# Another order of the first nine pieces and their products in the opening of a matmul with layer norm

## The chip, the core and the metric

The kernel runs on one core of one Trainium2 chip. The metric is the device time of one execution in microseconds (us); lower is better. Its engines are named as the profile names them: PE is TensorE (PEld its weight loads), DVE is VectorE, ACT is ScalarE, POOL is GpSimd, SP is SyncE, which here only issues DMAs.

## What is computed

`a` and `b` are 2048 x 2048, single precision; `gamma` and `beta` have 2048 elements.

```python
x = np.matmul(a, b)
mean = np.mean(x, axis=-1, keepdims=True)
var = np.var(x, axis=-1, keepdims=True)
normalized = (x - mean) / np.sqrt(var + eps)
return (gamma * normalized + beta).astype(np.float32)
```

## The kernel before, in words

The output is cut into 16 row tiles of 128 rows and 4 column quarters of 512. The contraction is cut into 16 k tiles of 128; four of them make a chunk. A product (`mm`, L85) is one 128x128 by 128x512 matmul in half precision, which adds one k tile to one bank of PSUM, the accumulator of one row tile and one quarter. In all there are 16 x 4 x 16 = 1024 products.

The single-precision inputs come by DMA from SP's queue into staging tiles (pool `stg`, six of them) and are cast to half precision by DVE: a piece of `a` (128 rows x 512 columns, 256 KB) by `load_a1` (L184 the DMA, L186 the cast), a piece of `b` (one k tile x one quarter, 256 KB) by `load_b1` (L198, L199), and doubled pieces of 512 KB by `load_a2` (L190, L194) and `load_b2` (L203, L205). Two single pieces share a staging tile, in the order in which they are loaded. SP waits, before a later load, until the staging tile is free and until the DMA eight places ahead of it has landed.

A piece of `a` has to be turned before it can be the stationary side of a product. `turn` (L243, L245) does four PE transposes of 128x128 into a bank of PSUM and one ACT copy from there into the tile `at`.

**The opening** works on the first five row tiles (R = 5) while the inputs come in. It takes quarter 0 of chunk 0 first (nine single pieces: A0 to A4 of `a`, B0 to B3 of `b`), then quarters 1 and 2 of chunk 0, then quarter 3 (`MAIN`) over all chunks, then the rest of quarters 0 to 2. The sums over chunk 0 of the first three quarters are copied out of PSUM by ACT (`put_aside`, L261) and added back later. After the opening, row tiles 5 to 15 are done one after the other: four quarters of 16 products each, with the layer norm of an earlier row on DVE beside them.

**What sets the order.** The kernel runs under a manual schedule: every engine does its instructions in the order in which the program calls them. The list `arrivals` sets the order of the nine DMAs on SP's queue and of their casts on DVE. The calls of `turn`, `mm` and `put_aside` set the order on PE and on ACT. In the kernel before, the arrivals are A0 B0 A1 A2 A3 A4 B1 B2 B3, and PE does, after the first row tile:

- turn row tiles 1, 2, 3 and 4, each as its piece arrives, and between them the products of k tile 0 for row tiles 1, 2 and 3
- k tile 1 for row tiles 0 to 3
- k tiles 0 and 1 for row tile 4
- k tile 2 for row tiles 0 to 4, then k tile 3 for row tiles 0 to 4; behind each product of k tile 3 ACT puts that row tile's sum aside

Before the first piece arrives, and in the first waits, PE multiplies zeros (`filler`, L236).

Of the kernel before, what the change touches and what calls it, by code (L numbers as in the profile page):

```python
# [16 lines left out]
def kernel(  # L17
# [19 lines left out]
    KC = 4  # L37
    KW = KC * P
    n_kc = n_kt // KC
    R = 5  # L40
# [32 lines left out]
    def bank(name):  # L73
        return psum.tile([P, NB], FP32, tag="ps", name=name)
# [4 lines left out]
    def at(i):  # L79
        return pair[i // 2][:, i % 2]  # L80

    def mm(i, q, kt, first, last):
        if (i, q) not in acc:
            acc[i, q] = bank(f"acc{i}_{q}")
        nc.tensor.matmul(  # L85
            acc[i, q], at(i)[:, kt, :], b16[:, kt, ds(q * NB, NB)],
            start=first, stop=last,
        )
# [71 lines left out]

    arrivals = [("a", 0), ("b", 0)] + [("a", i) for i in range(1, R)]
    arrivals += [("b", k) for k in range(1, KC)]

    a16_of = {}
    fresh = {"st": 0}
# [66 lines left out]
    def filler(n, to=None):  # L234
        for _ in range(n):
            nc.tensor.matmul(warm if to is None else to, zeros[:, 0:P], zeros, start=True, stop=True)  # L236

    def turn(rows, c):
        n = len(rows)
        t_ps = psum.tile([P, n, KC, P], FP16, tag="ps", name=f"tps{rows[0]}_{c}")  # L240
        for m, i in enumerate(rows):
            for j in range(KC):
                nc.tensor.transpose(t_ps[:, m, j, :], a16_of[i, c][:, ts(j, P)], ident)  # L243
        i0 = rows[0]
        nc.scalar.copy(  # L245
            pair[i0 // 2][:, ds(i0 % 2, n), ds(c * KC, KC), :], t_ps)
# [10 lines left out]
    def put_aside(p, q):  # L257
        if xs[p] is None:
            xs[p] = xpool.tile([P, N], FP32, tag="x", name=f"x{p}")
            bnst[p] = stat.tile([P, n_nb, 6], FP32, tag="bnst", name=f"bnst{p}")  # L260
        nc.scalar.copy(xs[p][:, ds(q * NB, NB)], acc.pop((p, q)))  # L261
# [11 lines left out]
    filler(1)  # L273
    turn([1], 0)
    filler(2)
    for i in range(2, R):
        turn([i], 0)
        mm(i - 1, 0, 0, True, False)
    for p in range(R - 1):
        mm(p, 0, 1, False, False)  # L280
    mm(R - 1, 0, 0, True, False)
    mm(R - 1, 0, 1, False, False)
    for kt in range(2, KC):
        for p in range(R):
            mm(p, 0, kt, False, kt == KC - 1)
            if kt == KC - 1:
                put_aside(p, 0)


    for q in ASIDE[1:]:  # L290
# [198 lines left out]
```

## Time and profile before

| | |
|---|---|
| device time, three runs | 245.38, 245.78, 245.42 us; median 245.42 us |
| the profiled execution's own time | 245.69 us |
| its span, first to last instruction | 243.70 us |
| so outside the span | 1.99 us |
| mean granted TensorE clock | 0.991 |
| DVE busy | 173.0 us (71%) |
| ACT busy | 55.1 us (23%) |
| DMA traffic in the opening's stretch 10 to 12 us | 383 GB/s |

Times inside an execution are counted from the span's start. A line of the timeline has the start, the duration, the engine, the line of the program, the operation with its tiles, and the number of merged instructions; what stands in brackets is the idle time of the engine before it and what ended it. The duration of a matmul is modelled and pipelined: a product of 512 columns is shown with 0.38 us, though the next one starts 0.22 us after it. So the start to start time is the one to count with. The chain of waits is the chain of work that ended last, in order of time.

### The profile page before, as it was taken

The page shows a single profiled execution, that of the slowest core. Times are in us where ns is not written, and L with a number is a line of the kernel's source. Part 1 is how long each engine was busy: PE and PEld are TensorE (multiplying, and loading weights), DVE is VectorE, ACT ScalarE, POOL GpSimd, SP SyncE. Part 2 cuts the span into 40 slices and gives each one's busy share as a digit, 9 for nine tenths or more (in the row PEclk, how much of TensorE's full clock was granted, in tenths as well). Part 3 has the DMA queues.
Part 4 walks back from the last instruction along what each step waited for, and adds up shares of the span by engine and source line. Part 5 has one row for each costly group of instructions (what it writes and reads, how often), then busy time and mean ns, then how long its engine had stood idle before and what let it go on. Part 6 is the DMA issues. An engine that isn't in the chain of part 4 may idle for free.

```text
span 243.7 us, 2983 instructions
## 1 busy us (share of the span) xinstructions
PE 235.0 (96%) x1137; PEld 108.3 (44%) x1137; DVE 173.0 (71%) x304; ACT 55.1 (23%) x104; POOL 12.6 (5%) x19
## 2 busy tenths in 40 slices
PE   6899999999999999999999999999999999999991
PEld 2344555444444444444444444444444444444440
DVE  1544454969997679999999995937558392946771
ACT  2466445500000011112121211112111121112132
POOL 0000000000210100000000000036000000000000
PEclk9999999999999999999999999999999999999996
DMA  4999999999999998888999797683907145120405
GB/s 122 393 389 384 384 350 392 386 335 370 360 266 204 150 139 242 237 186 251 241 224 256 143 290 177 192 202 74 256 5 180 78 115 146 58 114 0 175 1 172
DMA packets 41190, 52.64 MB, mean 216 GB/s; under 512 B 24404, under 2 KB 24404, under 8 KB 40920
## 3 DMA queue, kind: packets, MB, share of 16 engines
q1 hardware_dynamic: 39592, 46.68, 59.1%
q0 software_dynamic: 1584, 5.77, 15.3%
q8 instruction: 9, 0.15, 0.3%
q14 instruction: 5, 0.04, 0.1%
HBM read 35.67 MB, written 16.78 MB: 215 GB/s over the span
## 4 chain that ended last, share of the span: by engine, by line
PE 93%; DMA 2%; ACT 1%; DVE 1%; SPq 0%; issue 0%
PE acc L85 91%; DMA st<-in_a_dram 2%; PE tps L243 2%; ACT x L408 1%; DVE bnst L373 0%; PE y L396 0%; DVE a16s L186 0%; PE warm L236 0%; SPq L198 0%; SPq L184 0%; PE ms_ps L391 0%; ACT mv_last L389 0%; DVE mv_last L388 0%; ACT lead L392 0%
## 5 line engine op out<-in xcount | busy, mean ns | idle before, releaser
L85 PE MATMUL acc<-b,at 128*128 128x512 f16 x1024 | 223.2, 379 | 1.0 <-DVE b L199 0.9
L85 PEld LDWEIGHTS <-at 128*128 128x128 f16 x1024 | 99.6, 98 | 119.3 <-ACT at L245 1.3
L96 DVE BATCH_NORM_STATS2 bnst<-x 128x6 f32<-128x512 f32 x48 | 32.9, 689 | 33.9 <-ACT x L95 33.8
L95 ACT COPY x<-acc 128x512 f32<-128x512 f32 x48 | 27.7, 588 | 108.8 <-PE acc L85 107.5
L117 DVE SCALAR_TENSOR_TENSOR x<-x,rstd,beta_b 128x512 f32<-128x512 f32 x62 | 43.8, 747 | 0.6
L111 DVE SCALAR_TENSOR_TENSOR x<-x,mv,gamma_b 128x512 f32<-128x512 f32 x60 | 42.0, 741 | 0.0
L205 DVE CAST b<-stb 128x1024 f16<-128x1024 f32 x30 | 20.4, 688 | 11.0 <-DMA stb<-in_b_dram 10.9
L106 ACT ACTIVATE sq<-ve 128x1 f32<-128x1 f32 x15 | 3.0, 203 | 51.1 <-DVE ve L104 51.1
L245 ACT COPY at<-tps 128x512 f16<-128x512 f16 (+1 forms) x14 | 10.6, 769 | 14.3 <-PE tps L243 14.0
L265 DVE TENSOR_TENSOR x<-acc,x 128x512 f32<-128x512 f32 x15 | 10.3, 685 | 3.3 <-PE acc L85 3.3
L345 POOL DMA_DIRECT2D a<-in_a_dram x11 | 6.4, 583 | 91.1 <-DMA at<-a 90.8
L266 DVE BATCH_NORM_STATS2 bnst<-x 128x6 f32<-128x512 f32 x15 | 10.4, 695 | 0.5
L261 ACT COPY x<-acc 128x512 f32<-128x512 f32 x15 | 7.6, 607 | 5.1 <-PE acc L85 5.1
L186 DVE CAST a16s<-st 128x512 f16<-128x512 f32 x8 | 3.4, 427 | 6.4 <-DMA st<-in_a_dram 6.2
L243 PE MATMUL tps<-ident,a16s 128*128 128x128 f16 x80 | 6.8, 220 | 0.9 <-DVE a16s L186 0.8
L236 PE MATMUL warm<-zeros 128*128 128x512 f16 x19 | 6.2, 462 | 1.2 <-DVE zeros L152 1.2
L243 PEld LDWEIGHTS <-a16s 128*128 128x128 f16 x80 | 5.2, 98 | 4.7 <-DVE a16s L186 2.6
L194 DVE CAST a16s<-sta 128x1024 f16<-128x1024 f32 x6 | 4.2, 694 | 4.1 <-DMA sta<-in_a_dram 3.4
L357 POOL TENSOR_SCALAR gb<-gb 1x1024 f32<-1x1024 f32 x2 | 5.5, 2764 | 0.0
L102 DVE BATCH_NORM_AGGREGATE mv<-bnst 128x2 f32<-128x24 f32 x15 | 4.0, 264 | 0.5
L236 PEld LDWEIGHTS <-zeros 128*128 128x128 f16 x19 | 2.0, 115 | 4.2 <-issue 2.6
L255 POOL COPY gate<-stb 128x1 f32<-128x1 f32 x1 | 0.2, 183 | 63.5 <-DMA stb<-in_b_dram 63.5
(31 smaller groups left out, 22.8 us busy)
## 6 DMA issues: line engine op xcount, KB each, us to landing
stb<-in_b_dram SPq DMA_DIRECT2D x30, 512.0 KB, 6.5
out_dram<-x SPq DMA_DIRECT2D x30, 512.0 KB, 3.0
a<-in_a_dram POOLq DMA_DIRECT2D x11, 512.0 KB, 6.7
sta<-in_a_dram SPq DMA_DIRECT2D x6, 512.0 KB, 6.3
st<-in_a_dram SPq DMA_DIRECT2D x8, 256.0 KB, 7.4
st<-in_b_dram SPq DMA_DIRECT2D x4, 256.0 KB, 6.6
gamma_b<-in_gamma_dram SPq DMA_DIRECT2D x1, 1024.0 KB, 7.2
beta_b<-in_beta_dram SPq DMA_DIRECT2D x1, 1024.0 KB, 9.2
```

The source lines that it names most:

```text
L85: nc.tensor.matmul(acc[i, q], at(i)[:, kt, :], b16[:, kt, ds(q * NB, NB)], start=first, stop=last,)
L95: nc.scalar.copy(xs[i][:, qs], acc[i, q])
L96: nc.vector.bn_stats(bnst[i][:, q, :], xs[i][:, qs])
L111: nc.vector.scalar_tensor_tensor(xs[i][:, qs], xs[i][:, qs], mv[:, 0:1], gamma_b[:, qs], AluOp.subtract, AluOp.mult)
L117: nc.vector.scalar_tensor_tensor(xs[i][:, qs], xs[i][:, qs], rstd, beta_b[:, qs], AluOp.mult, AluOp.add)
L205: nc.vector.tensor_copy(b16[:, k:k + 2, ds(q * NB, NB)], st)
L236: nc.tensor.matmul(warm if to is None else to, zeros[:, 0:P], zeros, start=True, stop=True)
L243: nc.tensor.transpose(t_ps[:, m, j, :], a16_of[i, c][:, ts(j, P)], ident)
L245: nc.scalar.copy(pair[i0 // 2][:, ds(i0 % 2, n), ds(c * KC, KC), :], t_ps)
L261: nc.scalar.copy(xs[p][:, ds(q * NB, NB)], acc.pop((p, q)))
L265: nc.vector.tensor_tensor(xs[p][:, qs], acc[p, q], xs[p][:, qs], AluOp.add)
L266: nc.vector.bn_stats(bnst[p][:, q, :], xs[p][:, qs])
```

## The change

The arrivals become A0 B0 A1 A2 A3 B1 B2 A4 B3: row tile 4's piece goes from the sixth to the eighth place, and B1 and B2 each come one place earlier. B3 stays ninth.

On PE, everything up to the product of row tile 2 with k tile 0 stays as it is. From there the new order is: k tile 1 for row tiles 0 to 2; k tiles 0 and 1 for row tile 3; k tile 2 for row tiles 0 to 2; the turn of row tile 4; k tile 2 for row tile 3; k tile 3 for row tiles 0 to 3, each put aside at once; and last the four products of row tile 4, which is then put aside. The number of products, transposes, copies, casts and DMAs is the same, and so is all that follows the chunk.

```diff
-    arrivals = [("a", 0), ("b", 0)] + [("a", i) for i in range(1, R)]
-    arrivals += [("b", k) for k in range(1, KC)]
+    arrivals = [("a", 0), ("b", 0)] + [("a", i) for i in range(1, R - 1)]
+    arrivals += [("b", 1), ("b", 2), ("a", R - 1), ("b", 3)]
...
-    for i in range(2, R):
+    for i in range(2, R - 1):
         turn([i], 0)
         mm(i - 1, 0, 0, True, False)
+    for p in range(R - 2):
+        mm(p, 0, 1, False, False)
+    for kt in (0, 1):
+        mm(R - 2, 0, kt, kt == 0, False)
+    for p in range(R - 2):
+        mm(p, 0, 2, False, False)
+    turn([R - 1], 0)
+    mm(R - 2, 0, 2, False, False)
     for p in range(R - 1):
-        mm(p, 0, 1, False, False)
-    mm(R - 1, 0, 0, True, False)
-    mm(R - 1, 0, 1, False, False)
-    for kt in range(2, KC):
-        for p in range(R):
-            mm(p, 0, kt, False, kt == KC - 1)
-            if kt == KC - 1:
-                put_aside(p, 0)
+        mm(p, 0, 3, False, True)
+        put_aside(p, 0)
+    for kt in range(KC):
+        mm(R - 1, 0, kt, kt == 0, kt == KC - 1)
+    put_aside(R - 1, 0)
```

## The prediction, made before the changed kernel ran

> **What bounds the kernel now.** I read the page first: which engine is busy, and who holds the chain that ended last.
>
> ```profile
> PE 235.0 (96%) x1137; PEld 108.3 (44%) x1137; DVE 173.0 (71%) x304; ACT 55.1 (23%) x104; POOL 12.6 (5%) x19
> ...
> PE 93%; DMA 2%; ACT 1%; DVE 1%; SPq 0%; issue 0%
> ```
>
> PE holds 93% of the chain. A busy PE alone proves little, so I went to the chain of waits in order of time (start, us, what), to see where PE begins to be the bound.
>
> ```profile
> 9.87 0.39 PE acc L85
> 10.26 0.29 PE tps L243 x4
> 10.54 14.68 PE acc L85 x67
> 25.22 0.45 PE tps L243 x8
> ...
> 38.72 195.77 PE acc L85 x907
> ```
>
> From 9.87 us on only PE stands in the chain until its last product. The last line gives the pace: 195.77 / 907 = 0.2158 us per product; eight transposes take 0.45 us, so the four of a turn 0.22. The waits on PE from 10 to 234 us list no wait over their limit. But 67 products at 0.2158 make 14.46 us, not 14.68, so small gaps hide in the first stretch. I read them from PE's timeline in narrow windows:
>
> ```profile
> 9.87 0.39 PE L85 MATMUL acc<-b,at 128*128 128x512 f16 x1
> 10.15 0.40 PE L243 MATMUL tps<-ident,a16s 128*128 128x128 f16 x4
> 10.53 0.39 PE L85 MATMUL acc<-b,at 128*128 128x512 f16 x1
> 10.82 0.38 PE L85 MATMUL acc<-b,at 128*128 128x512 f16 x1
> ...
> 14.27 0.59 PE L85 MATMUL acc<-b,at 128*128 128x512 f16 x2
> ```
>
> These are row tile 2's product with k tile 0 (9.87), the turn of row tile 4 (10.15), row tile 3's product with k tile 0 (10.53), the first product of k tile 1 (10.82), and the first of quarter 1 (14.27), with which the changed stretch is over. What each waited for is in DVE's timeline, the casts of A3, A4, B1, B2, B3 and of the first doubled piece:
>
> ```profile
> 8.97 0.43 DVE L186 CAST a16s<-st 128x512 f16<-128x512 f32 x1 [0.24 <-DMA st<-in_a_dram]
> 9.66 0.43 DVE L186 CAST a16s<-st 128x512 f16<-128x512 f32 x1 [0.26 <-DMA st<-in_a_dram]
> 10.33 0.43 DVE L199 CAST b<-st 128x512 f16<-128x512 f32 x1 [0.25 <-DMA st<-in_b_dram]
> 11.01 0.43 DVE L199 CAST b<-st 128x512 f16<-128x512 f32 x1 [0.25 <-DMA st<-in_b_dram]
> 11.67 0.43 DVE L199 CAST b<-st 128x512 f16<-128x512 f32 x1 [0.23 <-DMA st<-in_b_dram]
> 13.03 0.69 DVE L205 CAST b<-stb 128x1024 f16<-128x1024 f32 x1 [0.93 <-DMA stb<-in_b_dram]
> ```
>
> DVE stands idle before each: landings set the pace, one piece per 0.66 to 0.69 us, while PE needs 0.2158 per product. The turn of row tile 4 starts 0.06 after A4's cast ends (10.09), k tile 1 starts 0.06 after B1's (10.76).
>
> **The change, step by step.**
>
> *What PE loses now.* From 9.87 to 14.27 are 4.40 us. In them start 18 products (row tiles 2 and 3 with k tile 0, 4 of k tile 1, 2 of row tile 4, 5 and 5 of k tiles 2 and 3) and one turn: 18 x 0.2158 + 0.22 = 4.11. So 0.29 us is idle, at three places: before the turn of row tile 4 (9.87 + 0.22 = 10.09, starts 10.15: 0.06), behind it, where row tile 3's product waits for ACT's copy of row tile 3 (10.15 + 0.22 = 10.37, starts 10.53: 0.16), and before k tile 1 (10.75 to 10.82: 0.07).
>
> *The moved loads.* Nine DMAs of 256 KB stay nine, in pairs on the same staging tiles; B3 stays ninth and alone, the tenth DMA waits for the same landing as now, and nothing behind is moved past anything. No trace shows a B piece as sixth. The steps between starts of casts are 0.67 and 0.69 (A to A), 0.67 (A4 to B1), 0.67 and 0.66 (B to B); the far row is A0 to B0 with 1.98 (4.94 to 6.93), which would make one piece 1.31 late, and the best row is 0.01 below 0.67. I take the row of the same switch in the running stream, A4 to B1: places six to nine keep their times, 9.66, 10.33, 11.01 and 11.67.
>
> *The new order, ready against needed* (ready is the cast's end plus 0.05):
> - B1 in the sixth place: 9.66 + 0.43 + 0.05 = 10.14; PE is free at 10.09. A wait of 0.06, the only one I find.
> - Row tile 3's copy: its product started at 10.53 as soon as it could; now it is needed at 10.14 + 3 x 0.2158 = 10.79. Cover 0.26.
> - B2: ready 10.82, needed after five products, 11.22. Cover 0.40.
> - A4, eighth: ready 11.01 + 0.48 = 11.49, needed at 11.87. Cover 0.38.
> - B3: ready 11.67 + 0.48 = 12.15, needed after the turn and one product, 11.87 + 0.22 + 0.22 = 12.31. Cover 0.15.
> - Row tile 4's weights: the turn starts at 11.87; ACT's copy started 0.43 after the turn before (10.15 to 10.58) and took 0.58: 12.88, plus 0.05 is 12.93. Needed after four products of k tile 3, 13.17. Cover 0.24.
> - Four products of row tile 4 end the chunk at 13.17 + 0.86 = 14.03, where the first doubled piece is ready (13.03 + 0.69 + 0.05 = 13.77). Cover 0.26.
>
> *Queued behind.* On ACT the copy of row tile 4 now stands just ahead of the puts aside. They start at about 12.88 instead of 13.60 (ACT's timeline) and, at 0.48 apart, four are done before 15. A bank from them is first needed at 14.03 + 6 x 0.2158 = 15.33. Nothing waits. On DVE and SP the order by place is the same.
>
> *Sum.* 14.03 against 14.27: the idle time falls from 0.29 to 0.06, a gain of 0.23 us. Does it reach the end? Behind 14.27 every wait by PE either moves with PE or is for a load. The load with the least cover that I found is `b`'s k tile 12 of quarter 3: the cast ends at 38.67 and PE comes at 39.20.
>
> ```profile
> 37.98 0.69 DVE L205 CAST b<-stb 128x1024 f16<-128x1024 f32 x1 [0.80 <-DMA stb<-in_b_dram]
> ...
> 39.20 0.38 PE L85 MATMUL acc<-b,at 128*128 128x512 f16 x1
> ```
>
> With 0.05 for the start, 0.48 of cover, of which the change uses 0.23. It holds. Against its own time the profiled execution would go from 245.69 to 245.46. The median of the runs shown is 0.27 below that execution, so the same gain is taken from it: 245.42 - 0.23 = **245.19 us**.
>
> *A rule against it.* All the products behind 10.82 start 0.2158 us apart. The Trainium skill (TensorE: Matmul & The Clock Gate, Back-to-back issue gap) gives about 131 ns per matmul of 512 columns as the sustained pace in a stream of weight loads and matmuls. By that figure PE would wait for the arrivals in both orders and be through with the chunk before 13.77 us, so that the sum would be no gain at all. The trace disagrees with it, with 0.2158 us over 907 products.
>
> **The rivals.**
>
> *The gain is eaten later: 245.42.* If the loads of the main stretch run 0.48 us later than in this profile, relative to PE, both kernels wait at k tile 12 for the same landing and the gain is gone; from 0.25 later on part of it goes. For it: the DMAs run full there. Against: the steps of the landings are steady within 0.03 us.
>
> *The cover of B3 is spent: slower.* Now B3 is ready at 12.15 and used at 13.19 (14.27 - 5 x 0.2158), a cover of 1.04; afterwards it is 0.15, with eight products behind it instead of five. A B3 that lands d us later costs the kernel before nothing up to d = 1.04 and the new one d - 0.15. From d = 0.39 on the change loses. One piece late, 0.67: 0.67 - 0.15 - 0.23 = 0.29 slower, 245.71. At the far row, 1.31 late: 246.35. For it: A0 to B0 shows that a piece of `b` can be 1.31 late. Against: that is the queue's start, and six steps behind it hold 0.67.
>
> *The arrivals set the end of the chunk: 245.42.* If a product took 0.18 us or less, the kernel before would have its 16 products behind 10.82 done when the first doubled piece is ready (10.82 + 16 x 0.18 = 13.70, ready 13.77), the new one too, and both would start quarter 1 there. Against: the pace of 0.2158 in the chain. This is what the page's figure would bring about.
>
> *More than forecast.* All the idle time that the order can reach is 0.29: 245.13.
>
> **How the numbers follow.** 0.2% is 0.49 us, about what a measurement of this kernel can tell from no change. The forecast is below it, and so is the gain of all idle time. Chances: forecast 0.78, gain eaten later 0.09, arrivals at the chunk's end 0.01, B3's cover spent 0.07, more than forecast 0.05. The runs shown lie 0.40 apart, so I add half of that, 0.20, at both ends: 245.13 - 0.20 = 244.93, and 245.42 + 0.20 = 245.62. The rival at 245.71 and above stays outside. Faster by over 0.2% (below 244.93) comes only from scatter on top of the gain: 0.09. Slower (above 245.91) needs B3 late by 0.87 us or more, or scatter: 0.06. Within: 0.85.
>
> **What would show it.** In PE's timeline k tile 1 starts at about 10.14, the turn of row tile 4 at 11.87, k tile 3 at 12.31, row tile 4's products at 13.17 and quarter 1 at 14.03. In the chain the stretch from about 10.14 to the next turn is gapless, and the turn that now starts at 25.06 comes at 24.83. The casts in DVE's timeline keep their starts by place. Wrong it would be if k tile 3 waits on its cast, if row tile 4's weights wait on ACT, or if quarter 1 starts at 14.03 and PE gives the 0.23 back before 39 us.

## The result, and the profile after

| | before | after |
|---|---|---|
| median of 22 runs each | 245.46 us | 245.09 us |
| lowest to highest | 245.20 to 246.50 | 244.93 to 245.36 |
| profiled execution, its span | 245.69, 243.70 | 245.19, 243.18 |

The ratio is 0.9984 with a 95% interval of 0.9978 to 0.9991: 0.39 us faster, between 0.22 and 0.54. That is under the 0.2% that the prediction set as its bound, 0.10 us below the forecast of 245.19, and inside its range.

The page's first and fourth part, as before:

```profile
PE 236.0 (97%) x1137; PEld 108.6 (45%) x1137; DVE 173.1 (71%) x304; ACT 55.0 (23%) x104; POOL 12.3 (5%) x19
...
PE 93%; DMA 2%; ACT 1%; DVE 1%; SPq 0%; issue 0%
```

They do not tell the two kernels apart. The chain of waits in order of time does (start, us, what):

```profile
7.34 0.44 DVE a16s L186
...
9.62 2.12 PE acc L85 x9
11.74 0.22 PE tps L243 x4
11.96 12.73 PE acc L85 x59
24.70 0.45 PE tps L243 x8
...
38.19 195.78 PE acc L85 x907
```

The chain before had a product, a turn, and then 67 products in 14.68 us, 0.22 more than 67 x 0.2158. Now nine products, the turn and 59 products follow each other almost without a gap: the nine take 1.96 from start to start (9.62 to the turn at 11.58; the 2.12 of the chain runs to the modelled end of the ninth), and the 59 take 12.73, which is 59 x 0.2158. The last line is the old one, 195.78 for 195.77: nothing changed behind the opening, and nothing of the gain was given back. The turn that started at 25.06 in PE's timeline comes 0.52 earlier, and so does the end of the span (243.70 to 243.18). This is more than the 0.23 of the forecast. DVE's timeline shows why, with the casts of A1, A2, A3, B1, B2, A4, B3 and the first doubled piece:

```profile
7.34 0.43 DVE L186 CAST a16s<-st 128x512 f16<-128x512 f32 x1 [0.26 <-DMA st<-in_a_dram]
8.07 0.43 DVE L186 CAST a16s<-st 128x512 f16<-128x512 f32 x1 [0.30 <-DMA st<-in_a_dram]
8.70 0.43 DVE L186 CAST a16s<-st 128x512 f16<-128x512 f32 x1 [0.20 <-DMA st<-in_a_dram]
9.37 0.43 DVE L199 CAST b<-st 128x512 f16<-128x512 f32 x1 [0.25 <-DMA st<-in_b_dram]
10.05 0.43 DVE L199 CAST b<-st 128x512 f16<-128x512 f32 x1 [0.25 <-DMA st<-in_b_dram]
10.72 0.43 DVE L186 CAST a16s<-st 128x512 f16<-128x512 f32 x1 [0.24 <-DMA st<-in_a_dram]
11.39 0.43 DVE L199 CAST b<-st 128x512 f16<-128x512 f32 x1 [0.25 <-DMA st<-in_b_dram]
12.76 0.69 DVE L205 CAST b<-stb 128x1024 f16<-128x1024 f32 x1 [0.94 <-DMA stb<-in_b_dram]
```

By place the steps are the old ones, 0.67 to 0.68 from the sixth to the ninth. But all of them stand 0.24 to 0.30 earlier than before, already A1 in the third place, which the change does not touch: 7.34, where the profile before has

```profile
7.64 0.43 DVE L186 CAST a16s<-st 128x512 f16<-128x512 f32 x1 [0.28 <-DMA st<-in_a_dram]
```

So 0.52 is two terms: some 0.29 of earlier landings, and the order's own 0.23. To part them I count from A1's cast. PE's timeline after, in narrow windows: k tile 1's first product, the turn of row tile 4, k tile 3, row tile 4's products, and quarter 1.

```profile
9.85 0.38 PE L85 MATMUL acc<-b,at 128*128 128x512 f16 x1
11.58 0.22 PE L243 MATMUL tps<-ident,a16s 128*128 128x128 f16 x1
12.02 0.38 PE L85 MATMUL acc<-b,at 128*128 128x512 f16 x1
12.88 0.38 PE L85 MATMUL acc<-b,at 128*128 128x512 f16 x1
13.74 0.38 PE L85 MATMUL acc<-b,at 128*128 128x512 f16 x1
```

Quarter 1 starts 13.74 - 7.34 = 6.40 behind A1's cast. Before it was 14.27 - 7.64 = 6.63. The forecast of 14.03 stood for 14.03 - 7.64 = 6.39.

### The profile page after: what moved, and what is told of

Same layout as the page of the kernel before. It is cut to its first block, busy times and chain, and to the rows that moved or that the text cites. A ratio compares the mean times of both kernels' runs of the same rounds, so it can differ in the third digit from the quotient of the medians.

```text
span 243.2 us, 2983 instructions
## 1 busy us (share of the span) xinstructions
PE 236.0 (97%) x1137; PEld 108.6 (45%) x1137; DVE 173.1 (71%) x304; ACT 55.0 (23%) x104; POOL 12.3 (5%) x19
## 4 chain that ended last, share of the span: by engine, by line
PE 93%; DMA 2%; ACT 1%; DVE 1%; SPq 0%; issue 0%
PE acc L85 91%; DMA st<-in_a_dram 2%; PE tps L243 2%; ACT x L413 1%; DVE bnst L378 0%; PE y L401 0%; ACT at L245 0%; DVE a16s L186 0%; PE warm L236 0%; SPq L198 0%; PE ms_ps L396 0%; SPq L184 0%; ACT mv_last L394 0%; DVE mv_last L393 0%; ACT lead L397 0%
## 5 line engine op out<-in xcount | busy, mean ns | idle before, releaser
L236 PE MATMUL warm<-zeros 128*128 128x512 f16 x19 | 7.4, 532 | 1.2 <-DVE zeros L152 1.2
```

## The experiments

Three theories were tried. **O**: the gain is PE's idle time at the sixth and seventh piece, and it takes loads and products moved together. **L**: the new order of the loads lets even the early pieces land sooner, which adds to the gain. **J**: the new order absorbs late landings that the old one passes on. For every run I give the start of quarter 1 counted from A1's cast (6.63 before, 6.40 after), which leaves L out, and the time, which takes it in. "The kernel before" beside a time is its median on the same chip in the same batch.

**Each half alone.** In the first run the list `arrivals` is the old one:

```diff
-    arrivals = [("a", 0), ("b", 0)] + [("a", i) for i in range(1, R - 1)]
-    arrivals += [("b", 1), ("b", 2), ("a", R - 1), ("b", 3)]
+    arrivals = [("a", 0), ("b", 0)] + [("a", i) for i in range(1, R)]
+    arrivals += [("b", k) for k in range(1, KC)]
```

> The new order on PE and ACT with the old order of the loads (A4 sixth, B1 seventh, B2 eighth). Theory O (the gain is the idle time that PE loses while it waits for the sixth and seventh piece, 0.23 us, and needs loads and products moved together): PE waits for B1 in the seventh place, 10.82 instead of 10.14, and for nothing else of weight, so quarter 1 starts at 14.71 by the times of the profile before: 0.44 us slower than the kernel before. Theory L (the new order of the loads lets every piece land sooner, already the early ones, and this is part of the gain): without the new loads A1's cast starts at about 7.64 as in the profile before. Theory J (beside O, the new order on PE absorbs late landings that the old one passes on): as O here, since B1 is waited for in full.

Measured: 245.97 us against 245.47, ratio 1.0014 (1.0001 to 1.0028). Quarter 1 at 14.53 - 7.46 = 7.07, where O said 14.71 - 7.64 = 7.07. L had A1's cast at about 7.64; it came at 7.46.

In the second the kernel before has the new list and nothing else.

> The new order of the loads with the old order on PE and ACT. Theory O: the turn of row tile 4 stands ahead of all of k tile 1 and waits for A4 in the eighth place, 11.49; behind it 18 products less one run without a gap, quarter 1 at 15.38: 1.11 us slower than the kernel before. Theory L: the same order on PE, but A1's cast starts near 7.34 as in the profile after, so 0.8 us slower. Theory J: as O.

Measured: 246.54 us against 245.47, ratio 1.0039 (1.0026 to 1.0052). Quarter 1 at 15.11 - 7.33 = 7.78; O said 15.38 - 7.64 = 7.74. Each half alone is a loss, as O has it. L's 0.8 does not come out, but A1's cast at 7.33 does.

**Half of the change.** B1 alone goes ahead of A4:

```diff
-    arrivals += [("b", 1), ("b", 2), ("a", R - 1), ("b", 3)]
+    arrivals += [("b", 1), ("a", R - 1), ("b", 2), ("b", 3)]
...
-    for p in range(R - 2):
+    turn([R - 1], 0)
+    for p in range(R - 1):
         mm(p, 0, 2, False, False)
-    turn([R - 1], 0)
-    mm(R - 2, 0, 2, False, False)
```

> Half of the change: B1 goes ahead of A4, B2 stays behind it; PE takes k tile 1 first, then the turn of row tile 4 as soon as A4 is there, then k tile 2. Theory O: PE is without a gap from the sixth piece on but for 0.05 before the turn, quarter 1 at 14.08: 0.19 us faster than the kernel before. Theory L: the gain hangs on how early the pieces land; if it comes from the order of the loads, it differs from the changed kernel's by more than 0.05. Theory J: a wait for A4 in the seventh place remains, so late landings cost as before, and the gain is nearer to 0.19 than to the 0.37 of the medians.

Measured: 245.18 us against 245.47, ratio 0.9982 (0.9969 to 0.9995). Quarter 1 at 13.88 - 7.43 = 6.45; O said 14.08 - 7.64 = 6.44. So by the profiles 0.18 of the order's 0.23 comes from B1 in the sixth place. By time it can't be told from the whole change (245.23 in the same batch). A1's cast stands at 7.43, between those of the two lists.

**Both kernels again**, with no edit: the changed one once, the one before twice.

> The changed kernel once more, for a second profile and more times. Theory O: quarter 1 starts 4.64 to 4.66 us after the start of A3's cast only if the pieces six to nine keep their steps (before: 14.27 less 8.97 is 5.30; after: 5.05), 0.23 to 0.25 less than before in each profile, while the start of A3's cast itself moves by up to 0.3 us from one execution to the next. Theory L: A1's cast starts near 7.34 again in every kernel with the new loads and near 7.64 in those with the old. Theory J: the time scatters less from run to run than that of the kernel before, and its gain by the medians is above 0.23.

The first pair of figures there is a slip; those in brackets are meant. Measured: 245.23 us against 245.47, ratio 0.9986 (0.9972 to 1.0000). Quarter 1 again at 13.74 - 7.34 = 6.40. By the medians the gain is only 0.24 here, against 0.37 in the result. J's other sign, less scatter, came out: 245.02 to 245.44 in 12 runs, where 35 of the kernel before in this batch spread from 245.02 to 247.19, and the table at the top shows the same. But the new loads under the old order on PE scatter as little (246.29 to 246.78, second run above), so this need not be J's cover.

> The kernel before once more, for a second profile. Theory O: quarter 1 starts 6.63 after A1's cast, whenever A1 lands; the start of A1's cast itself scatters and may be 7.33 as in the profiles with the new loads. Theory L (the new order of the loads makes the early pieces land sooner, which adds to the gain): A1's cast at 7.46 or later, as in the two profiles with the old loads and no further DMA, 7.64 and 7.46, against 7.33 to 7.43 in four with the new ones.

> The kernel before a third time, for the same question: theory O lets A1's cast be anywhere between 7.3 and 7.65, with quarter 1 at 6.63 behind it; theory L at 7.46 or later.

Measured: 245.56 and 245.44 us against 245.47, ratios 1.0006 (0.9993 to 1.0019) and 0.9995 (0.9984 to 1.0006). Quarter 1 at 14.08 - 7.46 = 6.62 and 14.07 - 7.46 = 6.61. These lines are from the timeline of the third profile of before, A1's cast and the first product of quarter 1:

```profile
7.46 0.43 DVE L186 CAST a16s<-st 128x512 f16<-128x512 f32 x1 [0.26 <-DMA st<-in_a_dram]
...
14.07 0.38 PE L85 MATMUL acc<-b,at 128*128 128x512 f16 x1
```

So the order's share is the same in every pair of profiles, 6.61 to 6.63 less 6.40: 0.21 to 0.23. A1's cast stands at 7.64, 7.46, 7.46 and 7.46 in the four profiles with the old list (the first run above among them) and at 7.34, 7.33 and 7.34 in the three with the new one. They do not overlap, which speaks for L with some 0.12 us; the first profile of before, at 7.64, was the latest of them all. The spans of the two later profiles, 243.50 and 243.52, less 243.18 are 0.32 to 0.34: 0.22 of O and 0.12 of L. The times can't confirm the 0.12: a median gain of 0.24 has hardly room for it, one of 0.37 has.

**B3 alone late.** B3 is loaded behind the first doubled piece, in both kernels:

```diff
-    for what in arrivals:
+    for what in arrivals[:-1]:
         (load_a1(what[1], 0) if what[0] == "a" else load_b1(what[1]))
-    for q in ASIDE[1:]:
-        load_b2(0, q)
-        load_b2(2, q)
+    load_b2(0, ASIDE[1])
+    load_b1(KC - 1)
+    load_b2(2, ASIDE[1])
+    load_b2(0, ASIDE[2])
+    load_b2(2, ASIDE[2])
```

> The kernel before with B3 loaded behind the first doubled piece instead of ahead of it, so that B3 alone comes later, ready about 1.36 us later than before, and quarter 1's first pair 0.67 us earlier. Theory O (the new order gains the idle time that PE loses at the sixth and seventh piece, and pays for it with the cover of B3, 0.15 instead of 1.04): k tile 3 waits 0.32 us, quarter 1 starts 6.95 after A1's cast instead of 6.63, 0.32 us slower than the kernel before. Rival (a late B3 matters little in either order, since what stands behind it in the queue is late too): no more than 0.1 slower.

Measured: 245.74 us against 245.47, ratio 1.0013 (1.0000 to 1.0027). Quarter 1 at 14.17 - 7.19 = 6.98.

> The changed kernel with B3 loaded behind the first doubled piece. Theory O: k tile 3 of row tiles 0 to 3 and all four products of row tile 4 stand behind B3; PE waits 1.20 us, quarter 1 starts 7.60 after A1's cast instead of 6.40, 0.97 us slower than the kernel before and 0.65 slower than it with the same loads: the sign of the change turns. Rival (as above): no more than 0.1 slower than the changed kernel, so still faster than the kernel before.

Measured: 246.38 us against 245.47, ratio 1.0029 (1.0012 to 1.0046). Quarter 1 at 14.92 - 7.29 = 7.63. PE's timeline of this run, the last product ahead of k tile 3 and the first of k tile 3:

```profile
11.76 0.38 PE L85 MATMUL acc<-b,at 128*128 128x512 f16 x1
13.20 0.38 PE L85 MATMUL acc<-b,at 128*128 128x512 f16 x1 [1.06 <-DVE b L199]
```

13.20 - 11.76 - 0.22 is a wait of 1.22 us for B3's cast; O said 1.20. With these loads the change is a loss of 0.64 us (246.38 less 245.74; O said 0.65), and 7.63 less 6.98 is 0.65 too. The sign of this change hangs on when B3 lands. Here A1's cast is at 7.19 with the old list and 7.29 with the new one, the other way round. So L is no fixed "A4 late makes A1 early"; it may hang on which pieces stand behind, which is not shown.

**A late queue.** One more DMA goes into the queue, ahead of the ninth piece (first two runs, n = 8) or of the seventh (last two, n = 6), in both kernels; `gamma_b` is overwritten later.

```diff
-    for what in arrivals:
+    for n, what in enumerate(arrivals):
+        if n == 8:
+            nc.sync.dma_start(gamma_b[0:64, 0:NB], a[ds((R + 1) * P, 64), 0:NB])
         (load_a1(what[1], 0) if what[0] == "a" else load_b1(what[1]))
```

> The kernel before with one more DMA of 128 KB (64 rows of 2 KB, into a part of a tile that is not in use yet) between the eighth and the ninth piece, so that B3 and all loads behind it land about 0.34 us later (half of the 0.67 us that 256 KB took). Theory O: B3 is ready at 12.49 and used at 13.19, and the later loads have covers of 0.48 and more: no change, quarter 1 starts 6.63 after A1's cast, time within 0.1 us of the kernel before. Theory J (the old order passes late landings on where the new one absorbs them): the same here, since the old order has the cover. Theory L (the order of the loads moves the early landings too): with the old order A1's cast starts later than the 7.33 to 7.34 of three profiles with the new one, at 7.46 to 7.64.

> The changed kernel with the same further DMA of 128 KB between the eighth and the ninth piece. Theory O with the prediction's cover of B3 of 0.15: PE waits 0.19 before k tile 3, quarter 1 starts 6.59 after A1's cast instead of 6.40; 0.05 us faster than the kernel before, and 0.05 than it with the same DMA: most of the gain is gone. Rival: if the cover of B3 were larger than the profile before let expect, the gain stays near 0.23. Theory L: A1's cast near 7.34.

Measured: 246.45 and 246.18 us against 245.54, ratios 1.0031 (1.0015 to 1.0047) and 1.0021 (1.0006 to 1.0036). Quarter 1 at 14.72 - 7.20 = 7.52 and 14.56 - 7.15 = 7.41. Every theory missed: O and J because the added DMA cost far more than 0.34 us, L because A1's cast came at 7.20 with the old list, where L had 7.46 or later (it came at 7.15 with the new list). B3's cast starts 5.41 and 5.21 behind A1's, instead of 4.04 and 4.05, so it is 1.37 and 1.16 late. What held up quarter 1 in the old kernel was then not B3 but the doubled piece behind it. These are DVE's and PE's lines of its chain of waits:

```profile
7.19 6.75 DMA stb<-in_b_dram
13.97 0.70 DVE b L205
14.72 10.96 PE acc L85 x50
```

Quarter 1 starts right behind that cast, 0.90 late (7.52 less 6.62). The new kernel waits for B3 at k tile 3 and is 1.01 late, as PE's timeline shows:

```profile
12.84 0.59 PE L85 MATMUL acc<-b,at 128*128 128x512 f16 x2 [0.61 <-DVE b L199]
```

So with the whole queue late the new order still ends 0.11 ahead by the profiles, but its B3 was 0.21 less late; with the old one's 1.37 it would be 0.10 behind (worked out, not run). By time the two can't be told apart: 0.27 by the medians, but the intervals overlap widely.

> The kernel before with the further DMA of 128 KB between the sixth and the seventh piece, so that B1, B2, B3 and all behind them land about 0.34 us later. Theory O and J: PE waits for B1 in full, quarter 1 starts 6.97 after A1's cast, 0.34 us slower than the kernel before. Theory L: A1's cast at 7.46 to 7.64.

> The changed kernel with the further DMA of 128 KB between the sixth and the seventh piece, so that B2, A4, B3 and all behind them land about 0.34 us later. Theory O and J: B2's cover of 0.40 and A4's of 0.38 take it, B3's of 0.15 does not: quarter 1 starts 6.59 after A1's cast, 0.05 us faster than the kernel before and 0.39 us faster than it with the same DMA; so a late seventh piece widens the gain from 0.23 to 0.39. Rival (the new order only saves the one wait and shields nothing): 0.34 slower than the changed kernel, the gain against the kernel with the same DMA stays 0.23. Theory L: A1's cast near 7.34.

Measured: 246.68 and 246.17 us against 245.54, ratios 1.0044 (1.0029 to 1.0059) and 1.0015 (0.9996 to 1.0035). The sizes missed again for the same reason: B3's cast is 1.33 and 1.17 late against A1's. Quarter 1 at 15.38 - 7.43 = 7.95, late by the whole 1.33, and 14.75 - 7.33 = 7.42, late by 1.02. The distance of the two grew from 0.22 to 0.53 us, by the medians to 0.51. Of this, 0.16 is that B3 was less late in the new kernel; with 1.33 in both the distance would be 0.37 (worked out, not run), where O and J had 0.39. J's direction is right: at a late seventh piece the new order has a cover and the old one has none. In the plain result no profile shows J at work: in none without the added DMA and with B3 ninth does a step between casts from the sixth to the ninth piece leave 0.66 to 0.69. But these are eight executions, and those without a profile scatter more in the kernel before, so that some of them may owe a loss to late landings stays open.

## Why the prediction was right, and where it was not

- **The idle time, 0.29 to 0.06.** Right. From row tile 2's first product to quarter 1 are 18 products and a turn, 4.11 us. Before it took 4.40, in the second profile of after 13.74 - 9.57 = 4.17. The first has 4.12, because A2's cast, 0.73 behind A1's instead of 0.67, made the stretch start late.
- **The covers.** Right to 0.01 where they show: B3's cast ends at 11.82, with 0.05 ready at 11.87, used at 12.02: 0.15. In the same way B2 has 0.40 (10.53, used at 10.93) and A4 has 0.38 (11.20, used at 11.58). The sums of the experiments that follow from the same table (7.07, 7.74, 6.44, 6.95, 7.60) came out at 7.07, 7.78, 6.45, 6.98 and 7.63.
- **The way to the end.** Right: from the first product of quarter 1 to the last product of the kernel it is 219.83 us in both kernels. The rival by which a later load eats the gain did not come: the cast for k tile 12 of quarter 3 now ends at 38.33, and PE comes at 38.68, 0.30 after it is ready.
- **"Places six to nine keep their times."** Only half right: they kept their steps, but the whole row of landings moved. The term that was missing in the sum is about 0.12 us, by four profiles against three. With it the sum is 0.22 + 0.12 = 0.34, beside a measured 0.39 (0.22 to 0.54); without it, 0.23 lies at the lower end of that interval. The measured 245.09 is also below 245.13, the most that the prediction let the order reach. That it is the order of the loads that does this rests on profiles alone, and the median gain of 0.24 in the second batch needs no such term. So the mechanism and 0.23 of the gain are shown, and what makes up the rest is open. So is how the order of the loads could move the early pieces: they are issued before the moved ones and at the same times.
- **The rival of B3's cover.** Its mechanism is real, and the run with B3 alone late gave its price. But the prediction counted B3 alone as late. In a late queue what stands behind B3 is late as well, and there the old order's cover was not 1.04 but that of the first doubled piece, 14.27 - 13.77 = 0.50. From the covers of the two orders (0.50 and 0.15) the new one can lose at most 0.35 on the old one by a late queue, 0.12 more than it gained. The prediction's price for the new order holds there too (B3 late by 1.16, less 0.15, is the measured 1.01); what it left out is that the old order loses as well.
- **The rule on the pace.** The Trainium skill's 131 ns per matmul (TensorE: Matmul & The Clock Gate, Back-to-back issue gap) would have made the gain nothing. The chain after shows 195.78 / 907 = 0.2159 us, and the gain is there.
- **What a measurement can tell.** The prediction took 0.49 us as about what a measurement of this kernel can tell from no change. The interval of the result, 0.22 to 0.54, tells a smaller gain, 0.39, from none.

## What to carry to other kernels

When landings pace an opening, list for each piece when it is ready and when it is first needed: the gain of another order is the idle time ahead of the last piece that is waited for, and it is bought with the covers of the pieces behind it. Move loads and products together; either half alone lost 0.5 to 1.1 us here. When such a list is tested for a late landing, shift everything behind the late piece too, and count from an event that both orders share, since the start of the row moves by itself: A1's cast by 0.18 between the profiles of the kernel before, nearly what the order is worth.

## What the runs showed that I had not expected

The added DMA of 64 rows of 2 KB was far dearer than half of one of 128 rows: the pieces behind it came 1.2 to 1.4 us later, instead of the 0.34 that its 128 KB take at the others' pace. In the first of these runs the DMA engines were as busy as ever (1.11, 1.12 and 1.00 in the stretches 9 to 10, 10 to 11 and 11 to 12 us), but they moved 303, 242 and 225 GB/s, where the third profile of before shows 402, 389 and 393. The Trainium skill says of two transfers to disjoint halves of the partitions that both spray over all 16 engines (DMA: Bandwidth & Descriptors, Rules for kernel authors). The full busy share does not speak against that; the bytes show that it is no price by size. B3's issue was late too in the first pair (6.47 instead of 5.07 in the kernel before), because as the tenth DMA it waits for B0's landing. That is not the whole of it: in the third run B1 was issued 0.62 later than in the third profile of before (4.42, 3.80) and cast 1.31 later (11.45, 10.14). Whether the half of the partitions, the rows read or something else makes this DMA dear was not tried.

A piece's landing also changed with what was queued behind it: with the added DMA ahead of the ninth piece, B1 and B2, issued before it, were cast 0.27 and 0.72 us later than without it, counted from A1 (2.95 and 4.07 instead of 2.68 and 3.35). It is the same kind of effect as the 0.12 us of L, though nothing here shows that it has the same cause.
